# Finishing the memory projection inside the first feed-forward block, and splitting the fourth group's weights earlier

## The chip, the cores and the metric

The kernel runs on one core of one Trainium2 chip. The metric is the device time of one execution, in microseconds (us). Five engines work side by side, each through its own list of instructions in order: TensorE does the matrix products (PE in the profile, PEld for its weight loads), VectorE (DVE) and ScalarE (ACT) do elementwise work, GpSimd (POOL) does a few small operations, and SyncE (SP) issues most of the transfers from memory.

## The reference

A two-layer decoder trunk over 256 tokens of width 1024. A memory of 256 rows is normalised and projected once, and four cross-attention heads of each layer read it:

```
mem_kv = rms_norm(mem, mem_norm_g) @ mem_w_kv          # 256 x 1024: 512 columns of keys, 512 of values
for i in range(2):
    x = x + 0.5 * swiglu(rms_norm(x, ffn1_norm_g[i]), ffn1_w_in[i], ffn1_w_out[i])
    hn = rms_norm(x, mix_norm_g[i])
    # layer 0: mLSTM heads, layer 1: sliding-window attention; both with memory heads beside them
    # memory heads: q and k normalised per head, softmax(q k^T) v
    x = x + concat(y_tok, y_mem) @ w_out
    x = x + 0.5 * swiglu(rms_norm(x, ffn2_norm_g[i]), ffn2_w_in[i], ffn2_w_out[i])
```

`rms_norm` is `x * rsqrt(mean(x*x) + 1e-6) * g`. The memory's keys and values are first needed by the mixer of layer 0, behind the first feed-forward block.

## The kernel before, in words

Everything is kept in float32 accuracy by splitting each operand into a high part and a rest (`wh`, `wl` for weights, `xh`, `xl` for activations) and doing three products, `mm3` (lines 227 to 229: high by high, then two mixed ones). A weight tile is 128 by 1024 numbers, 512 KB. SP loads it into `wr` (line 220, five buffers), ACT casts it into `wh` (line 213), and DVE subtracts to get `wl` (line 214). One weight tile feeds 24 matmuls. Activations are split with their gain in the same way (`split_gain`: ACT line 134, DVE line 243).

A norm is applied after the product, since its factor is one number per token: `Norm.square` and `Norm.fold` sum the squares (ACT and DVE), `Norm.chain` sums over partitions by two small matmuls with `onesr` (line 303) and then takes the reciprocal root, for the memory's norm as two diagonals on DVE (line 294) and a power on POOL (line 308), for the residual's as a chain of operations on DVE (lines 314 to 322).

`memory()` runs first. It multiplies the memory, not yet normalised, by the key and value weights in four column groups of 256 (`Group` with `rows=True`): groups 1 and 2 give keys, groups 3 and 4 give values. In the kernel before, the memory's squares are taken while group 2 runs, the sum matmuls stand in group 3, and then, ahead of group 4, come the finishing steps: `head_norm` for both key groups straight from their PSUM banks, the copy of group 3 scaled by the norm (`vM`, line 134), and the split and squares of the residual `xT` (`x0.put`). Group 4's scaled copy follows. The keys are turned by four transposes a group (`turn`, line 238) and copied to `kT` (line 449). Then `ffn()` multiplies by the first feed-forward weights: 11 groups, each of four weight tiles and 96 matmuls; `hidden` reads the finished banks once `x0`'s norm is there (lines 501 to 504).

The order on PE and SP is that in which the program is written, with `Weave` slotting the spawned chains in when its own clock reaches their due time (the numbers in `LAT`). ACT and DVE are ordered by a list scheduler; `tc.issue_after(last[0].ins)` tells it to put instructions behind the last weight cast issued so far. PSUM has eight banks, taken in turn by `mo()`.

Of the kernel before, what the change touches and what calls it, by code (L numbers as in the profile page):

```python
# [10 lines left out]
F32 = mybir.dt.float32  # L11
# [3 lines left out]
AF = mybir.ActivationFunctionType  # L15
ALU = mybir.AluOpType
# [3 lines left out]
P = 128  # L20
# [12 lines left out]
def constants():  # L33
# [16 lines left out]

LAT = dict(pieces=1, norm=8.5, mnorm=3.5, x0=17.0, mkeys=7.2, cross=9.5, cross_s=1.5,
           cross_m=3.7, cross_p=8.7, cross_o=3.0, gates=20.0, scores=2.2, scores_m=8.4, num=6.9, num_r=7.5,
           keys=5.5, keys_d=7.2, query=9.0, head=1.5, head_m=2.5, head_p=9.3, head_o=4.0)

# [42 lines left out]
def tile_trunk(ctx: ExitStack, tc: tile.TileContext, a, out):  # L99
    nc = tc.nc  # L100
    seq = [0]

    def mk(pool, shape, dt, tag):
        seq[0] += 1
        return pool.tile(shape, dt, tag=tag, name=f"{tag}_{seq[0]}")
# [7 lines left out]
    wv = Weave()  # L113
# [19 lines left out]
    def act(*args, **kw):  # L133
        ins = nc.scalar.activation(*args, **kw)  # L134
        if args[2] not in (AF.Copy, AF.Square):
            tabled[0] = ins
# [6 lines left out]
    def unit(dt):  # L143
        return mk(up, [P, 2, T], dt, "u")

    def tmp():
        return mk(tp, [P, 2, T], F32, "t")
# [4 lines left out]
    def mo():  # L152
        return mk(pb8, [P, 512], F32, "bank")
# [47 lines left out]
    def g(i):  # L201
        return gcol[:, i:i + 1]


    pieces = [1]
    last = [None]
# [11 lines left out]
    def wtile(src, nk, ncol=256):  # L218
        raw = mk(wrp, [P, nk, ncol], F32, "wr")
        nc.sync.dma_start(raw, src)  # L220
        return split(raw, [P, nk, ncol])

    def wcols(w, c0, kh):
        return wtile(w.rearrange("(k p) f -> p k f", p=P)[:, kh * 4:(kh + 1) * 4, c0:c0 + 256], 4)
# [16 lines left out]
    def split_gain(src, gc, hi, lo):  # L241
        act(hi, src, AF.Copy, scale=gc)
        nc.vector.scalar_tensor_tensor(out=lo, in0=src, scalar=gc, in1=hi.bitcast(F32),
                                       op0=ALU.mult, op1=ALU.subtract)
# [9 lines left out]
    class Norm:  # L254
# [4 lines left out]
            self.done = False  # L259
            self.xT, self.xh, self.xl = [], [], []  # L260

        def put(self, xn):
            c2 = len(self.xT)
            hi, lo = mk(xhp, [P, 2, T], F32R, "xh"), mk(xlp, [P, 2, T], F32R, "xl")
            for m in range(2):
                split_gain(xn[:, m], g(self.gi + 2 * c2 + m), hi[:, m], lo[:, m])
            self.xh.append(hi)
            self.xl.append(lo)
            self.xT.append(xn)
            self.square(xn, c2 == 0)  # L270
            if c2 == 3:
                self.fold()

        def square(self, xn, first):
            if first:
# [108 lines left out]
    def head_scales(zc, hd, scaled):  # L384

        s2 = 1.0 / hd if scaled else 1.0
        e = mk(sp, [P, 2], F32, "qsc")
        nc.vector.tensor_scalar(e, zc, EPS / s2, None, op0=ALU.mult)
        return 1.0 / (hd * s2), e

    def head_factor(src, n, hsc):

        hd = src.shape[2] // n
        sq, v, u = tmp(), col(), col()
        sqv = sq[:, :, :n * hd]
# [26 lines left out]
    vM = mk(cst, [P, 2, 512], F32, "vM")  # L422
    x0 = Norm(G_F1)

    def memory():

        idle = tmp().rearrange("p a b -> p (a b)")[:, :T].bitcast(BF16)
        nc.vector.memset(idle, 0.0)
        bank = mo()
        for i in range(WARM):  # L430
            nc.tensor.matmul(bank, idle[:, :P], idle, start=True, stop=True, skip_group_check=True)
        wkv = a["mem_w_kv"]
        mh, ml, wfirst = [], [], []
# [12 lines left out]
        norm = Norm(G_MEM, rows=False)  # L446

        def keys(gi, kr):
            nc.scalar.copy(kT[gi], turn(kr))
            return  # L450
            yield

        for gi in range(2):
            gr = Group(wkv, gi * 256, mh, ml, rows=True)
            for kh in range(2):
                if gi == 0 and kh == 0:
                    yield from gr.first_part(wfirst[0])
                else:
                    yield from gr.part(kh, wfirst[kh] if gi == 0 else None)
            if gi == 0:  # L460
                first = gr
                continue
            nc.sync.dma_start(con, a["con"])
            with tc.issue_after(last[0].ins):
                for c2 in range(4):
                    norm.square(memT[c2], c2 == 0)
            norm.fold()
            wv.spawn(norm.chain(), LAT['mnorm'])
            gv = Group(wkv, 512, mh, ml, rows=True)
            yield from gv.all()  # L470
            for c2 in range(4):
                nc.sync.dma_start(xT[c2], a["xT"][:, 2 * c2:2 * c2 + 2])
            yield norm.ready
            hsc = head_scales(norm.zc, P, False)
            for i, q in enumerate((first, gr)):
                kr = tmp()
                head_norm(kr, q.ps, 2, hsc)
                wv.spawn(keys(i, kr), LAT['mkeys'] + 1.5 * i)
        for gi in range(2):
            if gi == 0:  # L480
                gr = gv
            else:
                gr = Group(wkv, 768, mh, ml, rows=True)
                yield from gr.all()
            for h in range(2):
                act(vM[:, h, gi * 256:(gi + 1) * 256], gr.ps[:, h], AF.Copy, scale=norm.rc[:, h:h + 1])
            if gi == 0:
                with tc.issue_after(last[0].ins):
                    for c2 in range(4):
                        x0.put(xT[c2])  # L490
                wv.spawn(x0.chain(), LAT['x0'])


    KG = [(0, 4), (4, 4), (8, 4), (12, 4), (16, 4), (20, 2)]
# [39 lines left out]
    def ffn(x, w_in, w_out, nxt=None, mid=None):  # L534
# [13 lines left out]
        for c2 in range(4):  # L548
# [25 lines left out]
            else:  # L574
                nxt.put(xn)
        wv.spawn(nxt.chain(), LAT['norm'])

# [15 lines left out]
    def cross_spawn(gr, gi, layer, hsc, ys):  # L593
# [5 lines left out]
        def queries():  # L599
# [456 lines left out]
```

## Time and profile before

| | |
|---|---|
| time, median of 3 runs | 1009.38 us (1009.06 to 1010.25) |
| profiled execution | 1010.58 us; its span, first to last instruction, 1008.7 us |
| busy time in the span | PE 996.2 us, PEld 978.1, DVE 664.4, ACT 531.0, POOL 29.7 |
| transferred | 182.70 MB |

The profiled execution is 1.9 us longer than its span; that is what lies around the instructions. Times in rows of the profile are counted from the span's start. "PEclk" is the granted TensorE clock as a share of full speed. A row of the timeline has the start, the length, the engine, the line, the operation, what it writes and reads, the shape, the count, and in brackets the idle time before it and what ended it.

### The profile page before, as it was taken

To read this page: it belongs to the slowest core of one execution; us is meant where nothing else is said; L and a number is where in the kernel's file an instruction comes from. 1 tells how busy PE (TensorE), PEld (TensorE's weight loads), DVE (VectorE), ACT (ScalarE), POOL (GpSimd) and SP (SyncE) were. 2 spreads that over 40 slices of the span, in tenths; PEclk is the share of its full clock that TensorE was granted. 3 is DMA by queue.
4 is the path that set the end of the run, shared out by engine and by line. 5 is a ranking of instruction groups with operands and counts; after the bars stand their busy time and mean duration, and the time that the engine had idled before them with its cause. 6 is when DMAs were issued, how large, how long until landed. Compare 5 with 4: busy or idle time off the path is not lost.

```text
span 1008.7 us, 20573 instructions
## 1 busy us (share of the span) xinstructions
PE 996.2 (99%) x8560; PEld 978.1 (97%) x8560; DVE 664.4 (66%) x1078; ACT 531.0 (53%) x779; POOL 29.7 (3%) x27
## 2 busy tenths in 40 slices
PE   8899999999999999999999999999999999999998
PEld 6899999999999999999999999999997899999998
DVE  6776665668766696666567665656777768666551
ACT  7654444446566464444445444455578755454440
POOL 1100000000100000000000000000132000000000
PEclk9999999999999999999999999999999999999999
DMA  9676656676634666665666666556641257666550
GB/s 307 197 250 197 195 180 195 185 190 194 189 126 136 185 191 199 190 195 180 198 193 201 201 192 191 186 180 200 205 148 50 88 157 223 193 192 187 187 168 22
DMA packets 173204, 182.70 MB, mean 181 GB/s; under 512 B 7124, under 2 KB 168328, under 8 KB 173112
## 3 DMA queue, kind: packets, MB, share of 16 engines
q1 hardware_dynamic: 171872, 179.60, 58.1%
q10 hardware_dynamic: 1016, 1.58, 0.5%
q8 instruction: 67, 1.10, 0.4%
q0 software_dynamic: 224, 0.22, 0.2%
q14 instruction: 25, 0.20, 0.1%
HBM read 180.32 MB, written 1.05 MB: 180 GB/s over the span
## 4 chain that ended last, share of the span: by engine, by line
PE 94%; ACT 2%; DVE 2%; DMA 1%; issue 0%; SPq 0%; POOL 0%; ACTq 0%; DVEq 0%
PE bank L227 30%; PE bank L229 30%; PE bank L228 30%; PE bank L233 2%; ACT u L134 1%; PE bank L238 1%; DMA wr<-in_mem_w_kv_dram 1%; DVE wl L214 1%; ACT wh L213 1%; PE bank L989 1%; DVE col L957 0%; PE bank L303 0%; DVE col L956 0%; SPq L435 0%; DVE u L248 0%
## 5 line engine op out<-in xcount | busy, mean ns | idle before, releaser
L214 DVE TENSOR_TENSOR wl<-wr,wh 128x1024 fp32r<-128x1024 f32 (+1 forms) x347 | 414.6, 1197 | 273.1 <-ACT wh L213 272.0
L213 ACT CAST wh<-wr 128x1024 fp32r<-128x1024 f32 (+1 forms) x347 | 356.7, 1032 | 389.8 <-PE bank L228 364.9
L227 PE MATMUL bank<-xh,wh 128*128 128x256 f32 x1544 | 427.8, 277 | 0.0
L228 PE MATMUL bank<-xl,wh 128*128 128x256 f32 x1544 | 426.4, 276 | 0.0
L229 PE MATMUL bank<-xh,wl 128*128 128x256 f32 x1544 | 426.4, 276 | 0.0
L227 PEld LDWEIGHTS bank<-xh,wh 128*128 128x128 f32 x1544 | 290.0, 188 | 0.1
L228 PEld LDWEIGHTS bank<-xl,wh 128*128 128x128 f32 x1544 | 289.9, 188 | 0.1
L229 PEld LDWEIGHTS bank<-xh,wl 128*128 128x128 f32 x1544 | 289.9, 188 | 0.0
L227 PE MATMUL bank<-u,wh 128*128 128x256 f32 x896 | 249.3, 278 | 0.0
L228 PE MATMUL bank<-u,wh 128*128 128x256 f32 x896 | 247.6, 276 | 0.0
L229 PE MATMUL bank<-u,wl 128*128 128x256 f32 x896 | 247.5, 276 | 0.0
L227 PEld LDWEIGHTS bank<-u,wh 128*128 128x128 f32 x896 | 168.2, 188 | 1.7 <-issue 1.7
L228 PEld LDWEIGHTS bank<-u,wh 128*128 128x128 f32 x896 | 168.3, 188 | 0.1
L229 PEld LDWEIGHTS bank<-u,wl 128*128 128x128 f32 x896 | 168.2, 188 | 0.0
L227 PE MATMUL bank<-wh,xh 128*128 128x256 f32 x208 | 59.6, 287 | 0.4 <-ACT t L982 0.4
L228 PE MATMUL bank<-wl,xh 128*128 128x256 f32 x208 | 57.9, 278 | 0.0
L229 PE MATMUL bank<-wh,xl 128*128 128x256 f32 x208 | 57.8, 278 | 0.0
L501 DVE TENSOR_TENSOR t<-bank,rb 128x256 f32<-128x256 f32 x88 | 36.4, 421 | 6.7 <-PE bank L229 6.7
L227 PEld LDWEIGHTS bank<-wh,xh 128*128 128x128 f32 x208 | 39.1, 188 | 1.1 <-ACT t L982 0.7
L228 PEld LDWEIGHTS bank<-wl,xh 128*128 128x128 f32 x208 | 39.0, 188 | 0.1
L229 PEld LDWEIGHTS bank<-wh,xl 128*128 128x128 f32 x208 | 39.0, 188 | 0.0
L134 ACT ACTIVATE u<-bank,col,col 128x256 f32<-128x256 f32 (+1 forms) x48 | 24.9, 530 | 15.2 <-DVE col L960 7.9
(180 smaller groups left out, 682.9 us busy)
## 6 DMA issues: line engine op xcount, KB each, us to landing
wr<-in_ffn_w_in_dram SPq DMA_DIRECT2D x176, 512.0 KB, 4.4
wr<-in_ffn_w_out_dram SPq DMA_DIRECT2D x80, 512.0 KB, 4.0
wr<-in_a_w_in_dram SPq DMA_DIRECT2D x28, 512.0 KB, 3.9
wr<-in_b_w_in_dram SPq DMA_DIRECT2D x14, 512.0 KB, 4.5
wr<-in_a_w_out_dram SPq DMA_DIRECT2D x12, 512.0 KB, 3.3
wr<-in_b_w_out_dram SPq DMA_DIRECT2D x12, 512.0 KB, 3.3
wr<-in_ffn_w_out_dram SPq DMA_DIRECT2D x16, 256.0 KB, 2.7
wr<-in_mem_w_kv_dram SPq DMA_DIRECT2D x7, 512.0 KB, 7.8
```

The lines of the kernel that those rows point to most:

```text
L134: ins = nc.scalar.activation(*args, **kw)
L213: last[0] = nc.scalar.copy(hi[:, i * n:(i + 1) * n], src[:, i * n:(i + 1) * n])
L214: tt(out=lo[:, i * n:(i + 1) * n], in0=src[:, i * n:(i + 1) * n], in1=hi[:, i * n:(i + 1) * n].bitcast(F32), op=ALU.subtract)
L227: nc.tensor.matmul(ps, wh, xh, start=start, stop=False, skip_group_check=True)
L228: nc.tensor.matmul(ps, wh, xl, start=False, stop=False, skip_group_check=True)
L229: nc.tensor.matmul(ps, wl, xh, start=False, stop=stop, skip_group_check=True)
L233: nc.tensor.matmul(ps, lhsT, rhs, start=start, stop=stop, skip_group_check=True)
L238: nc.tensor.transpose(ps, src, ident[:k, :k])
L501: tt(out=t[:, m], in0=ps[m][:, :T], in1=x.rb, op=ALU.mult)
L989: nc.tensor.matmul(o[es[e], cs], vr[:, i, js], pTs[e][:, src], start=i == 0, stop=i == 1, skip_group_check=True)
```

## The change

The finishing steps leave `memory()`'s run of four groups. Each group's bank is now copied raw, without any scale, by ACT (`late`): key groups into two `raw` tiles, value groups into `vM`. Group 4's two weight tiles are requested and split ahead of the residual's splits, which are then issued behind group 4's weight casts. The residual's squares and norm (`sums`), and the memory's squares, norm, scaling of `vM` in place, head norms of the keys and their transposes (`finish`) are chains of their own, slotted in while the first feed-forward block runs. `put` gets a flag to leave out the squares. Fifteen lines are added in all, so that lines 281 and up have other numbers after (285 is 286, 303 is 304, 501 is 516); lines 134 to 247 and 238 keep theirs.

```
-LAT = dict(pieces=1, norm=8.5, mnorm=3.5, x0=17.0, mkeys=7.2, cross=9.5, cross_s=1.5,
+LAT = dict(pieces=1, norm=8.5, mnorm=8.0, mrest=6.0, finish=18.0, raw=4.0, x0=2.5, fold=5.0, mkeys=7.2, cross=9.5, cross_s=1.5,
...
-        def put(self, xn):
+        def put(self, xn, square=True):
...
-            self.square(xn, c2 == 0)
-            if c2 == 3:
-                self.fold()
+            if square:
+                self.square(xn, c2 == 0)
+                if c2 == 3:
+                    self.fold()
...
+        def late(raw, gr):
+            with tc.issue_after(last[0].ins):
+                nc.scalar.copy(raw, gr.ps)
+            return
+            yield
+
+        def sums():
+            for c2 in range(4):
+                x0.square(xT[c2], c2 == 0)
+                yield 1.5
+            x0.fold()
+            yield LAT['fold']
+            yield from x0.chain()
+
+        def finish(raw):
+            for c2 in range(4):
+                norm.square(memT[c2], c2 == 0)
+                yield 2.0
+            norm.fold()
+            yield LAT['mnorm']
+            yield from norm.chain()
+            yield LAT['mrest']
+            for h in range(2):
+                nc.vector.tensor_scalar(vM[:, h], vM[:, h], norm.rc[:, h:h + 1], None, op0=ALU.mult)
+            hsc = head_scales(norm.zc, P, False)
+            for i in range(2):
+                yield 3.0
+                kr = unit(F32)
+                head_norm(kr, raw[i], 2, hsc)
+                wv.spawn(keys(i, kr), LAT['mkeys'])
+
-        for gi in range(2):
+        raw = [unit(F32) for _ in range(2)]
+        for gi in range(4):
             gr = Group(wkv, gi * 256, mh, ml, rows=True)
+            wts = [wcols(wkv, 768, kh) for kh in range(2)] if gi == 3 else wfirst if gi == 0 else [None] * 2
+            if gi == 3:
+                with tc.issue_after(last[0].ins):
+                    for c2 in range(4):
+                        x0.put(xT[c2], False)
             for kh in range(2):
                 if gi == 0 and kh == 0:
-                    yield from gr.first_part(wfirst[0])
+                    yield from gr.first_part(wts[0])
                 else:
-                    yield from gr.part(kh, wfirst[kh] if gi == 0 else None)
...
-            with tc.issue_after(last[0].ins):
                 for c2 in range(4):
-                    norm.square(memT[c2], c2 == 0)
-            norm.fold()
-            wv.spawn(norm.chain(), LAT['mnorm'])
...
-            yield norm.ready
-            hsc = head_scales(norm.zc, P, False)
-            for i, q in enumerate((first, gr)):
-                kr = tmp()
-                head_norm(kr, q.ps, 2, hsc)
-                wv.spawn(keys(i, kr), LAT['mkeys'] + 1.5 * i)
...
-            for h in range(2):
-                act(vM[:, h, gi * 256:(gi + 1) * 256], gr.ps[:, h], AF.Copy, scale=norm.rc[:, h:h + 1])
-            if gi == 0:
-                with tc.issue_after(last[0].ins):
-                    for c2 in range(4):
-                        x0.put(xT[c2])
-                wv.spawn(x0.chain(), LAT['x0'])
+                    yield from gr.part(kh, wts[kh])
+            dst = raw[gi] if gi < 2 else vM[:, :, (gi - 2) * 256:(gi - 1) * 256]
+            wv.spawn(late(dst, gr), LAT['raw'])
+            if gi == 1:
+                nc.sync.dma_start(con, a["con"])
+            if gi == 2:
                 for c2 in range(4):
-                    nc.sync.dma_start(xT[c2], a["xT"][:, 2 * c2:2 * c2 + 2])
...
+        wv.spawn(sums(), LAT['x0'])
+        wv.spawn(finish(raw), LAT['finish'])
```

The change shows in the order of instructions up to the end of the first feed-forward block's first product; behind that, the order on PE, ACT and DVE is the same before and after.

ACT before, around the casts of group 4's weights (`wh_464`, `wh_494`); `t_403` and `t_412` are squares of the key banks 200 and 249, `vM_128` the scaled copy of group 3:

```order
L134 ACTIVATE xh_439<-u_107,gcol_99 128x256 x2
L134 ACTIVATE xh_448<-u_108,gcol_99 128x256
L134 ACTIVATE t_403<-bank_200 128x512
L134 ACTIVATE xh_448<-u_108,gcol_99 128x256
L134 ACTIVATE vM_128<-bank_326,rc_382 128x256 x2
L213 CAST wh_464<-wr_462 128x1024
L134 ACTIVATE t_412<-bank_249 128x512
L213 CAST wh_494<-wr_492 128x1024
L213 CAST wh_528<-wr_526 128x1024
```

ACT after, in the same place: `wh_383` and `wh_389` are group 4's weights, `u_201` the raw copy of key bank 251, `acc_498` to `t_597` the residual's squares:

```order
L456 COPY u_201<-bank_251 128x512
L134 ACTIVATE acc_498<-u_105 128x512
L134 ACTIVATE t_531<-u_106 128x512
L134 ACTIVATE t_564<-u_107 128x512
L134 ACTIVATE t_597<-u_108 128x512
L213 CAST wh_383<-wr_381 128x1024
L247 CAST u_633<-acc_498 128x256
L213 CAST wh_389<-wr_387 128x1024
L134 ACTIVATE xh_393<-u_105,gcol_99 128x256 x2
L134 ACTIVATE xh_399<-u_106,gcol_99 128x256 x2
L134 ACTIVATE xh_405<-u_107,gcol_99 128x256 x2
L134 ACTIVATE xh_411<-u_108,gcol_99 128x256 x2
```

The residual's splits and the scaled copy have gone behind group 4's casts, the key squares are gone from here, and a raw copy and the residual's squares stand ahead of the casts. The next ACT rows after are the raw copy of group 3 and the first feed-forward cast, `wh_470`.

DVE after, from the sums of the residual's squares to the first feed-forward tile's rest, `wl_471` (group 4's are `wl_384`, `wl_390`; before, `wl_465` stood behind the memory's diagonals, both `L398`-`L399` steps of the first key group and `L408`, which waits for POOL):

```order
L282 TENSOR_TENSOR acc_498<-acc_498,t_531 128x512
L282 TENSOR_TENSOR acc_498<-acc_498,t_564 128x512
L282 TENSOR_TENSOR acc_498<-acc_498,t_597 128x512
L286 SCALAR_TENSOR_TENSOR acc_498<-acc_498 128x256
L214 TENSOR_TENSOR wl_384<-wr_381,wh_383 128x1024
L248 TENSOR_TENSOR u_633<-acc_498,u_633 128x256
L214 TENSOR_TENSOR wl_390<-wr_387,wh_389 128x1024
L243 SCALAR_TENSOR_TENSOR xl_394<-u_105,gcol_99,xh_393 128x256 x2
L243 SCALAR_TENSOR_TENSOR xl_400<-u_106,gcol_99,xh_399 128x256 x2
L243 SCALAR_TENSOR_TENSOR xl_406<-u_107,gcol_99,xh_405 128x256 x2
L243 SCALAR_TENSOR_TENSOR xl_412<-u_108,gcol_99,xh_411 128x256 x2
L214 TENSOR_TENSOR wl_471<-wr_468,wh_470 128x1024
```

What moved: no DVE row here waits for POOL or for a matmul of the memory's norm any more, and the whole split of the residual stands behind `wl_390`.

PE before, the transposes of the first key group; 24 matmuls of the first feed-forward product stand ahead of them:

```order
L228 MATMUL bank_525<-xl_431,wh_528 128x256
L229 MATMUL bank_525<-xh_430,wl_529 128x256
L238 MATMUL bank_556<-con_109,t_402 128x128 x4
L227 MATMUL bank_524<-xh_422,wh_564 128x256
L228 MATMUL bank_524<-xl_423,wh_564 128x256
```

PE after, the same transposes; 516 matmuls of the first feed-forward product stand ahead of them, and 36 more ahead of those of the second key group:

```order
L228 MATMUL bank_1204<-xl_400,wh_1238 128x256
L229 MATMUL bank_1204<-xh_399,wl_1239 128x256
L238 MATMUL bank_1254<-con_109,u_1134 128x128 x4
L227 MATMUL bank_1205<-xh_393,wh_1238 128x256
L228 MATMUL bank_1205<-xl_394,wh_1238 128x256
```

The first transposes moved back by 492 matmuls. The residual's sum matmuls (line 303, now 304) stand behind 168 of that block's matmuls instead of behind 108, and the memory's, which stood in group 3, now behind 348.

More of the change, by code (lines that the diff above doesn't have):

```diff
@@ L458, in memory @@
                 else:
-                    yield from gr.part(kh, wfirst[kh] if gi == 0 else None)
-            if gi == 0:
-                first = gr
-                continue
-            nc.sync.dma_start(con, a["con"])
-            with tc.issue_after(last[0].ins):
-                for c2 in range(4):
-                    norm.square(memT[c2], c2 == 0)
-            norm.fold()
-            wv.spawn(norm.chain(), LAT['mnorm'])
-            gv = Group(wkv, 512, mh, ml, rows=True)
-            yield from gv.all()
@@ L471, in memory @@
-            for c2 in range(4):
-                nc.sync.dma_start(xT[c2], a["xT"][:, 2 * c2:2 * c2 + 2])
-            yield norm.ready
-            hsc = head_scales(norm.zc, P, False)
-            for i, q in enumerate((first, gr)):
-                kr = tmp()
-                head_norm(kr, q.ps, 2, hsc)
-                wv.spawn(keys(i, kr), LAT['mkeys'] + 1.5 * i)
[L479 to L484, printed above, removed]
-            for h in range(2):
-                act(vM[:, h, gi * 256:(gi + 1) * 256], gr.ps[:, h], AF.Copy, scale=norm.rc[:, h:h + 1])
-            if gi == 0:
-                with tc.issue_after(last[0].ins):
-                    for c2 in range(4):
-                        x0.put(xT[c2])
-                wv.spawn(x0.chain(), LAT['x0'])
+                    yield from gr.part(kh, wts[kh])
@@ L494, in tile_trunk @@
+            dst = raw[gi] if gi < 2 else vM[:, :, (gi - 2) * 256:(gi - 1) * 256]
[3 more added lines that the diff above has]
+            if gi == 2:
+                for c2 in range(4):
+                    nc.sync.dma_start(xT[c2], a["xT"][:, 2 * c2:2 * c2 + 2])
+        wv.spawn(sums(), LAT['x0'])
+        wv.spawn(finish(raw), LAT['finish'])
     KG = [(0, 4), (4, 4), (8, 4), (12, 4), (16, 4), (20, 2)]
```

## Prediction

> **What bounds the kernel now.** I read the page first: busy time, then the chain that ended last.
>
> ```profile
> PE 996.2 (99%) x8560; PEld 978.1 (97%) x8560; DVE 664.4 (66%) x1078; ACT 531.0 (53%) x779; POOL 29.7 (3%) x27
> PE 94%; ACT 2%; DVE 2%; DMA 1%; issue 0%; SPq 0%; POOL 0%; ACTq 0%; DVEq 0%
> ```
>
> TensorE is the bound, and the change takes no matmul away. It can gain only where PE stands still or runs slowly. So next: PE's waits from 27.4 to 60 us, its timeline there, and the granted clock in neighbouring stretches of 3.41 us (columns: length, busy us and count of PE, PEld, DVE, ACT, POOL, then PEclk).
>
> ```profile
> PE bank L227 <- ACT wh L213: 2.0, 1, 2.0
> PE bank L228 <- DVE wl L214: 1.5, 1, 1.5
> ...
> 17.50 0.28 PE L229 MATMUL bank<-wh,u 128*128 128x256 f32 x1
> 23.15 0.28 PE L229 MATMUL bank<-wh,u 128*128 128x256 f32 x1
> 29.04 0.28 PE L229 MATMUL bank<-wh,u 128*128 128x256 f32 x1
> 31.29 0.39 PE L227 MATMUL bank<-wh,u 128*128 128x256 f32 x1 [1.98 <-ACT wh L213]
> 33.16 0.39 PE L228 MATMUL bank<-wl,u 128*128 128x256 f32 x1 [1.48 <-DVE wl L214]
> 40.22 0.28 PE L229 MATMUL bank<-wh,u 128*128 128x256 f32 x1
> 40.33 0.28 PE L227 MATMUL bank<-xh,wh 128*128 128x256 f32 x1
> 40.68 0.28 PE L227 MATMUL bank<-xh,wh 128*128 128x256 f32 x1
> ...
> 10.25:13.66 3.41, 1.88 (x12) 1.47 (x12) 2.43 (x5) 2.74 (x5) 0.00 (x0) 1.00 1.08 389
> 13.66:17.07 3.41, 3.41 (x18) 3.41 (x18) 3.41 (x5) 3.09 (x6) 0.00 (x0) 0.50 1.09 390
> 27.31:30.73 3.42, 2.00 (x18) 1.80 (x16) 2.44 (x10) 1.26 (x3) 1.56 (x2) 1.00 0.00 0
> 30.73:34.14 3.41, 1.37 (x9) 1.17 (x10) 2.86 (x4) 3.41 (x5) 0.52 (x1) 1.00 0.00 0
> 34.14:37.55 3.41, 3.41 (x18) 3.41 (x18) 2.51 (x5) 3.41 (x6) 2.49 (x2) 0.50 0.81 231
> ```
>
> Groups 1, 2 and 3 of the memory end with the matmuls that start at 17.50, 23.15 and 29.04. Group 4 should go on at 29.16, but its cast comes at 31.29 and its rest at 33.16. From 34.14 to 37.55 the clock is then half: 18 matmuls touch that stretch, where 31 would fit. The first feed-forward matmul starts at 40.33, that is 11.17 us for 48 matmuls. At 0.118 each (29.04 to 29.16 by its neighbours, and 4.83 us for 41 in the pace rows below) they take 5.65. So this place costs 5.5 us, of which 3.5 are the two waits and some 1.6 the half clock. The same table shows when the clock drops: a stretch in which PE was busy 1.88 or 1.37 of 3.41 us is followed by half clock, one with 2.00 is not.
>
> The Trainium skill ("TensorE: Matmul & The Clock Gate", the section on the HAM clock gate) puts the return to half rate behind an idle window of about 3.4 us. The stretch of 3.41 us and the factor 0.50 agree, but here stretches that were 40% and 55% busy sufficed. By the page's rule the spell at 34.14 would not come from these waits and would stay: the forecast below would be 1.6 us higher.
>
> **The change, part by part.** Durations come from the same execution. ACT, then DVE:
>
> ```profile
> 15.75 1.66 ACT L134 ACTIVATE t<-u 128x512 f32<-128x512 f32 x3
> 17.31 1.99 ACT L213 CAST wh<-wr 128x1024 fp32r<-128x1024 f32 x2
> 20.27 0.41 ACT L247 CAST u<-acc 128x256 fp32r<-128x256 f32 x1 [0.97 <-DVE acc L285]
> 20.58 0.91 ACT L134 ACTIVATE xh<-u,gcol 128x256 fp32r<-128x256 f32 x2
> 22.28 2.10 ACT L134 ACTIVATE xh<-u,gcol 128x256 fp32r<-128x256 f32 x5
> 24.27 0.58 ACT L134 ACTIVATE t<-bank 128x512 f32<-128x512 f32 x1
> 40.53 0.84 ACT L134 ACTIVATE vM<-bank,rc 128x256 f32<-128x256 f32 x2 [2.52 <-PE bank L229]
> ...
> 9.34 1.67 DVE L243 SCALAR_TENSOR_TENSOR u<-u,gcol,u 128x256 fp32r<-128x256 f32 x4
> 16.49 2.28 DVE L281 TENSOR_TENSOR acc<-acc,t 128x512 f32<-128x512 f32 x3
> 19.82 0.42 DVE L285 SCALAR_TENSOR_TENSOR acc<-acc 128x256 f32<-128x256 f32 x1
> 20.15 1.22 DVE L214 TENSOR_TENSOR wl<-wr,wh 128x1024 fp32r<-128x1024 f32 x1
> 31.89 1.22 DVE L214 TENSOR_TENSOR wl<-wr,wh 128x1024 fp32r<-128x1024 f32 x1
> ```
>
> Instructions of one engine overlap a little, so I go from start to start: a square takes 0.52 (15.75 to 17.31 for three), a cast of a tile 0.95, an `xh` piece 0.40 (22.28 to 24.27 for five), a copy of a bank 0.48 (0.58 less the tenth that the others overlap), a sum's cast 0.31 (20.27 to 20.58). A reader of a bank begins 0.03 after the last matmul's end (40.22 + 0.28, ACT at 40.53); a matmul 0.05 after its `wl` (31.89 + 1.22 = 33.11, matmul at 33.16).
>
> The raw copies are a new wait: each stands in ACT's queue until PE ends its group, and everything behind it waits too. The first starts at 17.50 + 0.31 = 17.81; behind it the casts of group 3 end at 20.3 and their rests on DVE (1.2 each) at 21.8, while group 3 begins at 23.27 and needs its second tile at 26.1: covered by 3 us. The second copy starts at 23.15 + 0.31 = 23.46. Then four squares (2.08) give 26.02, and the cast `wh_383` ends at 27.07; group 4 needs it at 23.27 + 48 x 0.118 = 28.92: covered by 1.8 us. On DVE the three sums start when the second square is done (25.1) and take 2.28, then the fold 0.33, so `wl_384` runs from 27.8 to 29.05. It is needed at 29.04 plus nothing: a wait of 0 to 0.2 us. Group 4's second tile: the cast of the folded sum waits for the fold (28.0) and takes 0.31, `wh_389` ends at 29.3, `wl_390` at 30.6, needed at 31.7. So the large wait goes.
>
> What is late next is the first feed-forward tile. Behind `wh_389` ACT does eight `xh` pieces (29.25 + 3.2 = 32.45) and the raw copy of group 3 (32.95); `wh_470` ends at 34.0 and DVE, done with the `xl` pieces (eight at 0.42 behind 30.5) at 33.85, does `wl_471` from 34.03 to 35.25. PE comes to the first feed-forward matmul at about 34.75, and the third, which reads `wl_471`, would start at 34.99; it starts at 35.29. Another tenth goes in refilling, as behind 33.16. The fourth matmul then starts at 35.5, where before it started at 40.68: a gain of 5.2 us. Both ends of that: 5.5 + 0.2 if neither wait shows, and 4.2 if ACT's or DVE's steps take a further microsecond. The memory's two sum matmuls, which stood in group 3, move into the later product and come off it: 0.23 us (the two at 53.59 below). The half clock at 34.14 goes with the waits: no stretch of 3.41 us is then left with under 2.9 busy. That at 13.66 stays, as nothing moves ahead of 17 us.
>
> Transfers are asked for in the same order; a `wr` buffer is freed by its `wl`, and `wl_384` and `wl_390` now come 3 us earlier than 31.89 and on, so the loads behind them are not late. Removed: two scaled copies on ACT (0.84 each) for two raw ones (0.6), nothing on the path. Added: two raw key copies, and `vM` times its factor on DVE, 128x512 twice. No row shows that operation; the nearest are 0.42 (L285, half as large) and some 0.76 (L281): 1 to 1.5 us, in the feed-forward block where DVE is two thirds busy.
>
> That block has to absorb all the finishing work. Its margins, counted from the fourth matmul at 35.5: the residual's sum matmuls come after 168 matmuls, at about 55; nine DVE steps as large as L285 (0.42 to 0.5 one behind the other), three `wl` that wait for freed buffers and the copies of the factor end at 62, the first `hidden` has read its banks at about 66, and PE needs those banks again at 288 matmuls, 69. The memory's sum is ready at 70, needed at 76; the first turned keys are ready at 87, needed at 96. So I cost them at nothing; with the cover gone, a PE wait there would be a few tenths to 3 us.
>
> **The pace of the matmuls.** There is a price that the order hides. PE's timeline, around the transposes and the residual's sum:
>
> ```profile
> 38.09 0.28 PE L229 MATMUL bank<-wh,u 128*128 128x256 f32 x1
> 42.92 0.28 PE L228 MATMUL bank<-xl,wh 128*128 128x256 f32 x1
> 43.16 0.60 PE L238 MATMUL bank<-con,t 128*128 128x128 f32 x4
> 46.10 0.28 PE L227 MATMUL bank<-xh,wh 128*128 128x256 f32 x1
> 53.47 0.28 PE L229 MATMUL bank<-xh,wl 128*128 128x256 f32 x1
> 53.59 0.39 PE L303 MATMUL bank<-u,onesr 128*128 128x256 f32 x2
> 53.81 0.28 PE L227 MATMUL bank<-xh,wh 128*128 128x256 f32 x1
> 256.45 0.28 PE L228 MATMUL bank<-wl,xh 128*128 128x256 f32 x1
> 731.88 0.60 PE L238 MATMUL bank<-con,u 128*128 128x128 f32 x4
> 732.44 0.28 PE L228 MATMUL bank<-wl,xh 128*128 128x256 f32 x1
> 733.38 0.28 PE L227 MATMUL bank<-wh,xh 128*128 128x256 f32 x1
> ```
>
> From 38.09 to 42.92 there are 41 steps, 0.1178 us each, all at full clock and with nothing waited for. From 46.10 to 53.47 there are 65, 0.1134 each. The long pace holds from the first group on and through both waits; the short one begins right behind the first four transposes at 43.16 and goes on, past the sum at 53.59, to 256.45. So in this trace the pace has two values that persist, and in the memory and the first feed-forward block only the transposes changed it. After the change the first transposes stand behind 516 feed-forward matmuls instead of 24: 492 matmuls at the long pace, 492 x 0.0044 = 2.15 us lost. The bounds of this term: 0 if the short pace begins at once, and all some 1880 matmuls from 43.5 to 256.5, 8.3 us, if the later transposes do not bring it. I take 2.15, since what ends the long pace in this block is one thing in the trace, and the sum at 27.5 us in group 3 did not.
>
> **Sum.** 5.2 - 0.23 - 2.15 = 2.8 us. The profiled execution becomes 1010.58 - 2.8 = 1007.8. It stood 1.2 above the median of the three runs, so against that median: 1009.38 - 2.8 = 1006.6 us, a ratio of 0.9972.
>
> **Rivals.** First, the short pace comes early, by the short wait at 35 or by the sum matmuls: then 0 to 0.6 us of the 2.15 are lost, and the time is 1004.4 to 1005.0. For it: the pace can be short for 200 us, past a sum. Against it: both long waits before (31.29 and 33.16) left it long at 38.09. Second, slower: the transposes at 516 and 552 leave the pace long, as those at 731.88 did, behind which 732.44 to 733.38 is eight steps of 0.1175. Then it stays until 256, 8.3 us are lost, and the time is 1009.38 - 4.97 + 8.3 = 1012.7. It decides from 1130 matmuls at the long pace on, that is if it lasts to about 170 us. Against it: those at 731.88 stood in a product with weights as the moving operand; the four at 43.16 stood in the very product that follows here, and there are two such sets. Third, half clock still comes between 29 and 38 us, as the page's rule would leave it, or because the short waits fall badly: 1.6 us more, 1008.2. The table of stretches speaks against it. Fourth, the finishing work delays the feed-forward block or the ACT chain ahead of group 4 by 1 to 2.5 us more than counted: 1007.6 to 1009.1, which is no change within what can be measured.
>
> **How the numbers follow.** The forecast has 62%, the early short pace 13%, the lasting long pace 8%, half clock 7%, delays 10%. About 0.2% (2.0 us) is what can be told from no change, so faster means under 1007.4 and slower over 1011.4. The forecast's own spread is about 0.8 us (the 4.2 to 5.7 of the first term, and the runs' own 1.2), which leaves some 54 of its 62 points under 1007.4; with the early pace and a little of the rest, faster has 68%. Slower is the lasting long pace, 8%; the same 24%. The range leaves out the lasting pace and the ends of the others: 1004.4 to 1009.0.
>
> **What would show it.** Right: PE goes from the memory's last group into the feed-forward block with under 1 us of waits, `PEclk` stays 1.00 from 20 us on, the fourth feed-forward matmul starts near 35.5, steps are 0.118 until the four transposes near 96 us and 0.113 behind them. Wrong: a step of 0.113 at 40 us already (then faster than said), or 0.118 at 150 us (slower); a wait of PE on `wl` above 0.5 us near 29 or 35; a wait on a bank near 69 us, or on the turned keys near 96.

## The result, and the profile after

| | before | after |
|---|---|---|
| time, median | 1009.82 us (1009.06 to 1010.80, 4 runs) | 1004.31 us (1003.73 to 1005.52, 4 runs) |
| ratio | | 0.9946 (0.9934 to 0.9958) |
| profiled execution | 1010.58 us, span 1008.7 | 1004.76 us, span 1003.0 |

The change made the kernel 5.5 us faster (4.2 to 6.7 by the interval), where 2.8 had been forecast. An execution can have spells of half clock (3.41 us each; the profile before has two, a first at 13.66 and one behind group 4's waits at 34.14), and which it has differs from run to run, so profiles with the same first spell are compared below too.

The page of after, its busy row, and PE's waits up to 300 us (engine and line, what it waited for, then us in total, times, longest):

```profile
PE 993.9 (99%) x8560; PEld 975.7 (97%) x8560; DVE 664.6 (66%) x1080; ACT 531.9 (53%) x779; POOL 29.4 (3%) x27
...
PE bank L432 <- DVE t L429: 1.4, 1, 1.4
PE bank L228 <- DVE wl L214: 0.9, 1, 0.9
PE bank L227 <- ACT wh L213: 0.4, 1, 0.4
```

The two waits of 2.0 and 1.5 us at group 4 are not in this list any more; the three that are left stand ahead of 14 us. Now the same stretches and the same places as before (stretches: length, busy us and count of PE, PEld, DVE, ACT, POOL, then PEclk, DMA share and GB/s):

```profile
9.83:13.24 3.41, 2.25 (x15) 1.66 (x13) 2.68 (x5) 2.32 (x5) 0.00 (x0) 1.00 1.08 388
13.24:16.65 3.41, 3.26 (x27) 3.26 (x28) 3.41 (x6) 2.13 (x3) 0.00 (x0) 1.00 1.08 388
30.31:33.72 3.41, 3.39 (x29) 3.18 (x28) 3.17 (x7) 3.35 (x6) 0.00 (x0) 1.00 0.61 184
20.00:250.00 230.00, 229.89 (x2016) 229.61 (x2015) 165.46 (x242) 128.56 (x165) 4.32 (x4) 1.00 0.68 206
```

```profile
27.40 0.28 PE L229 MATMUL bank<-wh,u 128*128 128x256 f32 x1
...
27.66 0.38 PE L228 MATMUL bank<-wl,u 128*128 128x256 f32 x1
...
33.30 0.28 PE L227 MATMUL bank<-xh,wh 128*128 128x256 f32 x1
33.42 0.28 PE L228 MATMUL bank<-xl,wh 128*128 128x256 f32 x1
33.81 0.38 PE L229 MATMUL bank<-xh,wl 128*128 128x256 f32 x1
34.03 0.28 PE L227 MATMUL bank<-xh,wh 128*128 128x256 f32 x1
34.50 0.28 PE L228 MATMUL bank<-xl,wh 128*128 128x256 f32 x1
53.35 0.28 PE L229 MATMUL bank<-xh,wl 128*128 128x256 f32 x1
53.47 0.40 PE L304 MATMUL bank<-u,onesr 128*128 128x256 f32 x2
53.94 0.28 PE L229 MATMUL bank<-xh,wl 128*128 128x256 f32 x1
60.17 0.28 PE L227 MATMUL bank<-xh,wh 128*128 128x256 f32 x1
93.38 0.60 PE L238 MATMUL bank<-con,u 128*128 128x128 f32 x4
```

Four readings. First, the fourth feed-forward matmul starts at 34.03, where it started at 40.68: 6.65 us earlier. Second, no stretch between 20 and 250 us is at half clock, and PE is busy for 229.89 of those 230 us: nothing that was moved into the feed-forward block makes PE wait. Third, this execution has no half clock at 13.24 either; the stretch ahead of it was 2.25 us busy, where before it was 1.88. Nothing that the change moved stands there, so this part of the gain is luck (the run of the changed kernel again, below, has that spell). Fourth, from 34.50 to 53.35 there are 160 steps of 0.1178 us, the long pace; from 53.94 to 60.17, behind the residual's sum matmuls at 53.47, there are 55 of 0.1133. So the long pace ended 40 us ahead of the transposes at 93.38.

Where DVE now stands ahead of the feed-forward block (start, length, engine, line, operation; in brackets the idle time before it):

```profile
26.39 1.22 DVE L214 TENSOR_TENSOR wl<-wr,wh 128x1024 fp32r<-128x1024 f32 x1
...
32.53 2.36 DVE L214 TENSOR_TENSOR wl<-wr,wh 128x1024 fp32r<-128x1024 f32 x2 [0.24 <-ACT wh L213]
```

The first row is `wl_384`, ready at 27.61, and the matmul that reads it starts at 27.66 with a wait of 0.02 us. The last is `wl_471` and the next: the first of them is ready at about 33.7, and the matmul at 33.81 started 0.27 us late for it (PE itself stood still for 0.11 of that, since the matmul before it ran until 33.70). Both are the small waits that the prediction had put there.

### The profile page after: what moved, and what is told of

It is laid out like the page before. It is cut to its first block, busy times and chain, and to the rows that moved or that the text cites. A ratio compares the mean times of both kernels' runs of the same rounds, so it can differ in the third digit from the quotient of the medians.

```text
span 1003.0 us, 20581 instructions
## 1 busy us (share of the span) xinstructions
PE 993.9 (99%) x8560; PEld 975.7 (97%) x8560; DVE 664.6 (66%) x1080; ACT 531.9 (53%) x779; POOL 29.4 (3%) x27
## 4 chain that ended last, share of the span: by engine, by line
PE 93%; ACT 3%; DVE 2%; DMA 1%; issue 0%; SPq 0%; ACTq 0%; DVEq 0%
PE bank L227 30%; PE bank L229 30%; PE bank L228 30%; PE bank L233 2%; ACT u L134 1%; PE bank L238 1%; ACT wh L213 1%; DMA wr<-in_mem_w_kv_dram 1%; DVE wl L214 1%; PE bank L1004 1%; ACT xh L134 0%; DVE col L972 0%; DVE acc L282 0%; PE bank L304 0%; DVE col L971 0%
```

## The experiments

What was open: why 5.5 us and not 2.8, that is what each part is worth, what the first half-clock spell has to do with it, and what ends the long pace (steps of 0.1178 us instead of 0.1133). The theory throughout: the gain is the waits and half clock around group 4 (5.2 us), less the matmuls moved off (0.23), less what the long pace costs, plus the chance of the first spell.

**The changed kernel again** (`after_again`), unchanged, beside the others.

> The changed kernel as it is, more runs of it. Theory 1: two kinds of runs about 1.5 us apart, the longer with a mean clock 0.002 lower; over more runs the gain on the kernel before comes down from 5.5 towards 4.3 to 4.8 us. Theory 2: it stays at 5.5 us.

Measured: 1005.70 us (1004.12 to 1006.39, 5 runs), ratio 0.9954 (0.9941 to 0.9968), that is 4.6 us; the medians of that comparison differ by 3.9 (1009.60 over 15 runs of the kernel before). Its profile caught the first spell:

```profile
10.10:13.51 3.41, 1.94 (x12) 1.32 (x11) 2.49 (x5) 2.81 (x6) 0.00 (x0) 1.00 1.08 389
13.51:16.92 3.41, 3.41 (x16) 3.41 (x17) 3.22 (x5) 1.65 (x2) 0.00 (x0) 0.50 1.09 389
...
35.63 0.29 PE L227 MATMUL bank<-xh,wh 128*128 128x256 f32 x1
54.95 0.28 PE L229 MATMUL bank<-xh,wl 128*128 128x256 f32 x1
55.07 0.40 PE L304 MATMUL bank<-u,onesr 128*128 128x256 f32 x2
```

This is the like-for-like pair to the profile before, which had that spell too. The fourth feed-forward matmul starts at 35.63 (forecast 35.5), 5.05 us earlier than before. From 35.63 to 54.95 there are 164 steps of 0.1178, and the sum at 55.07 ends the long pace again. The spans differ by 1008.7 - 1004.6 = 4.1 us.

**Filling the first wait**, in the kernel before (`fill_before`) and in the changed one (`fill_after`): five more of the kernel's 512-column warm-up matmuls around the first matmul of group 1's second tile, where PE waits for its rest (the row at 13.10 below shows what is left of that wait).

```
+        def fill(n):
+            for i in range(n):
+                nc.tensor.matmul(bank, idle[:, :P], idle, start=True, stop=True, skip_group_check=True)
...
                     yield from gr.first_part(wts[0])
+                    fill(2)
...
+                    yield from gr.part(kh, wts[kh], (lambda: fill(3)) if gi == 0 else None)
```

The function handed to `part` is called inside `mm3`, behind the first matmul of the tile.

> The kernel before, with five more warm-up matmuls (512 columns, 0.22 us each) put where PE waits at 11.4 to 13.3 us for group 1's second weight tile, two ahead of the tile's first matmul and three behind it. They feed nothing. Theory 1 (the half-clock spell at 13.66 us of the before profile is a matter of how the free stretches of 3.41 us fall on those two waits; it belongs to neither kernel, and the change is worth 5.2 - 0.23 - 0.63 = 4.3 us): the spell never comes, so this kernel runs at the fast end of the kernel before, 1008.5 to 1009.4 us, with a small spread. Theory 2 (the change itself is worth the whole 5.5 us that the medians show, without such luck): no change of the median beyond 0.4 us, 1009.4 to 1010.2.

> The changed kernel with the same five matmuls. Theory 1: the profile of the changed kernel had no such spell, so nothing is gained against its fast runs: 1003.7 to 1004.8 us, and 4.0 to 4.7 us under the kernel before with the same fill. Theory 2: 5.5 us under the filled kernel before.

Measured: `fill_before` 1009.29 us (1008.52 to 1010.67, 11 runs), ratio 0.9999 (0.9990 to 1.0008); `fill_after` 1003.99 us (1003.73 to 1004.23, 5 runs), ratio 0.9944 (0.9931 to 0.9956). In the changed kernel the fill did what was meant: all five runs have a mean clock of 1.000 and lie within 0.5 us, where five of the changed kernel alone lay within 2.3. In the kernel before the spread stayed at 2 us, which was not expected; four of its eleven runs show a mean clock of 0.996 or 0.997, where one spell makes 0.998. The idle end of a run can be at half clock too (in the profile before from 1006.94 to 1008.70, worth about 0.001), so the one run at 0.997 may have one spell or two; the three at 0.996, by this estimate, have two. Where the second lies no profile shows; the one taken is of a run at 0.998, with one spell, from 31.4 us. A rival to the wait at 11 to 13 us is group 4's place itself. That is an estimate from this profile: two neighbouring stretches that begin at 25.70 and 29.11 would be only 1.57 and 1.79 us busy there, which could make two spells behind those waits alone.

So theory 1 held for `fill_after` by itself (1003.7 to 1004.8), but not for the small spread of `fill_before`, and not for the difference of the two: the filled medians lie 5.3 us apart, where 4.0 to 4.7 was forecast. The difference from the forecast's 4.3 is in part the pace: in the profile of `fill_after` it is short from the start of the feed-forward block, which is worth 0.6 us against the changed kernel. The profile of `fill_after` (timeline, then stretches):

```profile
11.46 0.61 PE L439 MATMUL bank<-t 128*128 128x512 bf16 x2
12.07 0.82 PE L439 MATMUL bank<-t 128*128 128x512 bf16 x3
13.10 0.39 PE L230 MATMUL bank<-wl,u 128*128 128x256 f32 x1 [0.21 <-DVE wl L214]
...
8.21:11.62 3.41, 3.39 (x21) 2.73 (x22) 3.06 (x7) 2.59 (x5) 0.00 (x0) 1.00 1.05 351
11.62:15.03 3.41, 3.20 (x22) 2.33 (x21) 3.21 (x5) 2.99 (x5) 0.00 (x0) 1.00 1.08 387
```

Both stretches are at least 3.2 us busy, and full clock follows. Its matmuls are at the short pace from 34.2 us on already.

**The hoist alone** (`hoist_only`): the kernel before, with group 4's two tiles split ahead of the head norms and the residual's splits, and nothing else moved.

```
+            w4 = [wcols(wkv, 768, kh) for kh in range(2)]
             yield norm.ready
...
-                yield from gr.all()
+                for kh in range(2):
+                    yield from gr.part(kh, w4[kh])
```

> The kernel before, with one part of the change alone: group 4's two weight tiles are requested and split ahead of the head norms and of the residual's splits; the finishing steps stay in the memory part, and the transposes stay early. Theory 1 (the rest of group 4's first tile waits on DVE behind a head norm that waits for POOL, and what is put behind comes late for the first feed-forward tile): PE still waits about 3 us for the first wl of group 4 (to about 32.4 us instead of 33.2) and then about 5 us for the first feed-forward wl (to about 43.8 us): 3 us slower than before, about 1012.5. Theory 2 (the weights' place is what gained, the finishing steps could have stayed): 3 to 5 us faster, 1005 to 1006.

Measured: 1013.94 us (1012.96 to 1015.46, 4 runs), ratio 1.0044 (1.0030 to 1.0058): 4.4 us slower, where theory 1 had 3. PE's waits from group 4 on, then DVE and two stretches:

```profile
PE bank L228 <- DVE wl L214: 2.9, 1, 2.9
PE bank L227 <- ACT wh L213: 1.9, 1, 1.9
PE bank L229 <- DVE wl L214: 0.8, 1, 0.8
...
28.95 0.69 DVE L408 TENSOR_TENSOR t<-bank,col 128x512 f32<-128x512 f32 x1 [1.12 <-POOL col L401]
29.56 1.22 DVE L214 TENSOR_TENSOR wl<-wr,wh 128x1024 fp32r<-128x1024 f32 x1
...
27.82:31.23 3.41, 0.52 (x5) 0.40 (x4) 2.29 (x4) 3.31 (x7) 1.00 (x1) 1.00 0.00 0
38.05:41.47 3.42, 0.81 (x4) 0.61 (x5) 3.10 (x6) 3.39 (x6) 0.00 (x0) 1.00 0.00 0
```

The rest of group 4's tile still stands behind the key heads' step that waits for POOL (28.95), so its wait is 2.9 us; and the residual's splits, now behind group 4's casts, make the first feed-forward tile 2.7 us late. The waits sum to 5.6 us where they were 3.5, and each of the two nearly empty stretches is followed by half clock (0.50 in the stretches from 31.23 and from 41.47). The finishing steps, not the order of the casts alone, held group 4 back.

**The finishing steps alone** (`finish_only`): the changed kernel with group 4's tiles split where `part` asks for them, behind the residual's splits.

```
-            wts = [wcols(wkv, 768, kh) for kh in range(2)] if gi == 3 else wfirst if gi == 0 else [None] * 2
+            wts = wfirst if gi == 0 else [None] * 2
```

> The changed kernel with the other part alone: the finishing steps stay in the feed-forward block, but the residual's splits stand ahead of group 4's weight casts, as in the kernel before. Theory 1 (most of the gain is that DVE no longer waits for POOL and for the memory's norm; the weights' place is worth what eight splits take on DVE less the slack): group 4's first wl comes about 1.5 us late instead of 0.02, the wait for the first feed-forward wl (0.27 us) is gone, so PE's fourth feed-forward matmul is 1.2 us later than in the changed kernel and the time 1005.2 to 1006.5, up to 1.6 us more in runs in which that wait brings a half-clock spell. Theory 2 (both parts are needed, neither gains by itself): 1008 us or more.

Measured: 1005.35 us (1004.84 to 1005.91, 4 runs), ratio 0.9955 (0.9939 to 0.9971).

```profile
27.90 0.38 PE L227 MATMUL bank<-wh,u 128*128 128x256 f32 x1 [0.21 <-ACT wh L213]
29.16 0.39 PE L228 MATMUL bank<-wl,u 128*128 128x256 f32 x1 [0.88 <-DVE wl L214]
```

The waits at group 4 come back at 1.1 us in all, the wait at the first feed-forward tile is gone, and no half clock follows. All four runs have a mean clock of 1.000; the changed kernel's four runs with 1.000 (of nine) have a mean of 1004.12. So beside the finishing steps the hoist is worth about 1.2 us, and without them it costs 4.4.

**What ends the long pace.** Six kernels, all from the changed one. `z_early`, `z_156`, `z_192`: the residual's sum matmuls stand behind 120, 156 or 192 feed-forward matmuls instead of 168 (`fold` in `LAT` 0.0, 3.0 or 8.0 instead of 5.0); `z_early_2` is `z_early` again, letter for letter. `pairs_rows` puts two spare matmuls of `onesr` by an activation ahead of group 3 and two behind the sixth feed-forward matmul, `single` one behind the sixth and three behind the 102nd, all into a bank that is overwritten afterwards:

```
+    def spare(ps, n, mv):
+        for i in range(n):
+            nc.tensor.matmul(ps, onesr, mv, start=True, stop=True, skip_group_check=True)
```

> The changed kernel with one number changed: the residual's sum matmuls (line 304) stand behind 120 feed-forward matmuls instead of 168. Theory P1 (two sum matmuls in a stream with activations moving end the long pace of 0.118 us; in a stream with weights moving they leave or bring the long one): steps are 0.118 until those two matmuls and 0.113 right behind them, 48 matmuls earlier, 0.2 us gained. Theory P2 (the pace is drawn anew, by chance of timing, at any break): it may change there or not. Theory P3 (the pace changes with time or with the block's progress, not with these matmuls): it still changes near 53.9 us, behind 168.

> The changed kernel with two pairs of extra matmuls by onesr (128x256, overwritten by the real products, nothing waits for them): one pair ahead of group 3 of the memory, where weights move, and one behind six matmuls of the first feed-forward group, where activations move. Theory P1: the pace stays 0.118 behind the first pair and is 0.113 from the second pair on, at about 34 us, so the fourth part of 1 us is lost less: 0.6 us gained, 0.47 us paid for the four matmuls. Theory P2: either pair may change it. Theory P3: no change before 53.9 us.

> The kernel with the residual's sum behind 120 feed-forward matmuls, once more. In its first profile the pace was long from 34 us on and stayed long past this sum, and changed at the memory's sum, behind 348. In all profiles so far, one weight load of three is 0.192 us long in the long pace and 0.188 otherwise. Theory P4: the sum ends the long pace where the long load is that of line 227, of line 304 or of line 229, and not where it is that of line 228; which one it is, is left by the last wait. P2: the pace behind a sum has nothing to do with that.

> The residual's sum behind 156 feed-forward matmuls. P4: short pace behind it, unless the long load is that of line 228. P2: either. P3 (the block's progress): no change before 168.

> The residual's sum behind 192 feed-forward matmuls. P4 as above; if the long pace ends there, it was long for 24 matmuls more than in the changed kernel (0.1 us). P3: the change comes at 168, ahead of the sum.

> The changed kernel with one extra matmul by onesr behind six feed-forward matmuls and three behind 102 (128x256, overwritten by the real products). Theory P4: each of them can end the long pace, by which load is the long one; one matmul does as well as two or three. Theory P5 (only two in a row with the same weights end it): the single one changes nothing, the three do.

One profiled execution each, so the times themselves decide nothing (one spell more or less outweighs what is looked for): `z_early` 1005.18, `pairs_rows` 1005.76, `z_early_2` 1005.48, `z_156` 1003.52, `z_192` 1004.12, `single` 1004.42 us. First PE in `z_early`, then in `z_early_2`:

```profile
34.11 0.28 PE L228 MATMUL bank<-xl,wh 128*128 128x256 f32 x1
47.30 0.28 PE L229 MATMUL bank<-xh,wl 128*128 128x256 f32 x1
47.42 0.40 PE L304 MATMUL bank<-u,onesr 128*128 128x256 f32 x2
47.90 0.28 PE L229 MATMUL bank<-xh,wl 128*128 128x256 f32 x1
60.50 0.28 PE L228 MATMUL bank<-xl,wh 128*128 128x256 f32 x1
74.52 0.40 PE L304 MATMUL bank<-u,onesr 128*128 128x256 f32 x2
```

```profile
35.94 0.28 PE L228 MATMUL bank<-xl,wh 128*128 128x256 f32 x1
48.63 0.28 PE L229 MATMUL bank<-xh,wl 128*128 128x256 f32 x1
48.75 0.39 PE L304 MATMUL bank<-u,onesr 128*128 128x256 f32 x2
```

In `z_early` the steps are 0.1178 before the sum at 47.42 (112 of them) and behind it (107 from 47.90 to 60.50), and they stay so until the memory's sum at 74.52. In `z_early_2`, the same program, 112 steps of 0.1133 lead to the same sum: the pace was short from the first wait of the feed-forward block on. It was short from there in `z_156`, `z_192` and `fill_after` too, and long in the profiles of `after`, `after_again`, `finish_only` and `z_early`. Behind that wait the pace takes about five steps to settle (in `z_156` 0.222, 0.118, 0.122, 0.116, 0.114, then 0.113). The spare matmuls behind the sixth feed-forward matmul, in `pairs_rows` at 35.87 and in `single` at 34.31, fall into that settling; the pace behind them is short, and whether they made it so is not shown. The first pair of `pairs_rows`, at 23.33 in group 3, left the pace long. In `fill_before` the sum in that group even began it: 0.1133 up to 25.35, 0.1176 behind it. So in the memory's groups the long pace is not a fixture either.

So a sum does not always end the long pace (it did not at 47.42), nor does a given amount of progress in the block. A third idea was that it depends on which of the three weight loads is the longer one, 0.192 us instead of 0.188, when the sum comes; it fits the six sums that were met in the feed-forward block while the pace was long, but the four last runs could not try it, since the pace was short before any sum came. In the memory's groups no load is the longer one in the long pace (187 to 188 ns each in `before` and `hoist_only`), so there the sign is missing. What chooses the pace behind a wait stays open. It is not the program alone, as `z_early` and `z_early_2` show.

**The parts together** (`best`): the changed kernel with the fill, with two spare matmuls behind the sixth feed-forward matmul, and with the third and fourth split of the residual behind the first feed-forward tile's cast.

```
-                    for c2 in range(4):
+                    for c2 in range(2):
                         x0.put(xT[c2], False)
...
                     wh, wl = wcols(w_in, part * FF + gi * 256, kh)
+                    if len(x.xh) == 2:
+                        with tc.issue_after(last[0].ins):
+                            for c2 in range(2, 4):
+                                x.put(xT[c2], False)
```

> A version meant to beat both: the changed kernel, with the five filling matmuls at 11 to 13 us, the pair by onesr behind six feed-forward matmuls, and the residual's third and fourth split put behind the first feed-forward tile's cast and rest, so that wl of that tile does not come late (0.27 us of wait and 0.1 of refill). Theory 1 and P1: the filled changed kernel (1003.99) less 0.35, and no more than 0.24 paid for the pair, since the pace there was short anyway: 1003.4 to 1004.1 us. If the third and fourth split come late instead, a wait near 39 us: 1004.5 us.

Measured: 1003.67 us (1003.39 to 1004.16, 5 runs), ratio 0.9941 (0.9928 to 0.9954).

```profile
32.80 0.29 PE L227 MATMUL bank<-xh,wh 128*128 128x256 f32 x1
33.04 0.28 PE L231 MATMUL bank<-xh,wl 128*128 128x256 f32 x1
33.49 0.39 PE L236 MATMUL bank<-xh,onesr 128*128 128x256 f32 x2
```

In `best` the third feed-forward matmul starts 0.24 us behind the first (0.51 in the changed kernel): the wait for `wl_471` is gone. The steps go from 0.118 to 0.113 at 33.15, three matmuls ahead of the spare pair at 33.49 and with no wait in front: here the pair did not end the long pace. The version has the lowest median of the versions with more than one run, by 0.6 us under the changed kernel's median in the first comparison and 0.3 under `fill_after`, which is within the spread of the runs.

## Why the prediction was wrong, point by point

The time, 1004.31, came out 0.1 below the range's low end and 2.3 below the forecast. The waits and the clock behind them were right; the term for the pace was mis-sized because its rule was wrong, and one outcome was taken as fixed that differs from run to run.

- **The waits and the half clock, 5.2 us: right.** In `after_again`, which has the first spell as the profile before has, the fourth feed-forward matmul came 5.05 us earlier. The small waits that were to be next came where and as large as said, and `finish_only` shows that the hoist is worth about 1.2 us of it.
- **The finishing work costs nothing: right.** PE stood still for 0.11 of 230 us from 20 us on. The fourth rival (delays) is out.
- **The half clock at 34 goes: right**, and the third rival is out: no profile of the changed kernel shows it. The Trainium skill's condition, an idle window ("TensorE: Matmul & The Clock Gate", the section on the HAM clock gate), is not what the rows show: 1.37, 1.88 and 1.94 of 3.41 us busy, none of them idle, were each followed by half clock. But the prediction's own reading, that the busy time of a stretch tells when the clock drops, does not hold either. In `z_early_2` 2.04 us busy was followed by half clock; in the kernel before 2.00 was not, and in `z_192` 1.78 was not (below first `z_early_2`, then `z_192`, each time the stretch and the one behind it; the stretches of `z_192` are counted back from the fall of its clock at 1001.14 us, in steps of 3.4133):

```profile
9.92:13.34 3.42, 2.04 (x13) 1.44 (x12) 2.60 (x6) 2.56 (x5) 0.00 (x0) 1.00 1.08 389
13.34:16.75 3.41, 3.41 (x16) 3.41 (x17) 3.26 (x5) 1.70 (x2) 0.00 (x0) 0.50 1.08 388
```

```profile
751.97:755.38 3.41, 1.78 (x15) 0.95 (x13) 2.70 (x13) 3.32 (x13) 0.00 (x0) 1.00 0.00 0
755.38:758.80 3.42, 3.42 (x27) 2.61 (x26) 2.27 (x10) 1.50 (x7) 0.00 (x0) 1.00 0.00 0
```

What the Trainium skill says in that section of a free-running window agrees with two profiles in which PE had the same two waits at 11 to 13 us: 0.58 and 0.88 in `after_again`, 0.57 and 0.88 in `z_156`. In the first one stretch, 10.10 to 13.51, holds both (1.94 busy) and half clock follows; in the second the stretches are cut at 12.31, are 2.83 and 2.53 busy, and no half clock follows. In `after` the first of these waits was shorter as well, 0.43.

- **The pace, 2.15 us: this step failed.** "In the memory and the first feed-forward block only the transposes changed it" was read off one trace, and "the sum at 27.5 us in group 3 did not" off one event in it. In the profiled execution of the changed kernel the residual's sum ended the long pace after 168 matmuls: (168 - 24) x 0.0044 = 0.63 us lost, not 2.15. In six profiles of the changed kernel's close variants (`fill_after`, `best`, `z_early_2`, `z_156`, `z_192`, `single`) the short pace stood within the block's first ten matmuls, and this term is near 0. In `hoist_only` the second set of transposes even began a long pace: six steps of 0.113 ahead of it, then 71 of 0.1178 from 47.76 to the sum at 56.12. What chooses the pace stays open. The first rival, an early short pace, was the right one in its mechanism; it had 13%, against 62% for the forecast. That its 1004.4 to 1005.0 us also came near is in part luck: it counted on the first spell, and the runs with that spell have a mean of 1005.83.
- **"That at 13.66 stays": only in some runs.** The nine runs of the changed kernel fall, by mean clock, into 4 at 1.000 (mean 1004.12 us), one at 0.999 (1004.57) and 4 at 0.998, that is with one spell (1005.83). Three of the four in the first comparison had none, so its 5.5 us lie on the high side. The 25 runs of the kernel before fall into 9 at 0.998, with one spell (1009.11), 7 at 0.996, with two (1010.16), and 9 at 0.997, which can be either (1010.07). Where the second spell lies is known from one profile alone, and `fill_before` has runs at 0.996 although the wait at 11 to 13 us is filled there. With one spell less in the changed kernel than before, runs differ by 1009.11 - 1004.12 = 5.0 us, or by 1010.16 - 1005.83 = 4.3; over all runs of both the gain is 1009.75 - 1004.93 = 4.8 us.

The account of the two profiles that both have the first spell (`before` and `after_again`): 5.05 for the waits and the half clock, -0.23 for the two matmuls moved off, -0.63 for the pace, 4.2 in all; their spans differ by 4.1.

## What to carry to other kernels

Price a wait on the bound engine together with the clock behind it: here 3.5 us of waits took another 1.6 through the stretch that followed. Splitting a tile earlier pays only if nothing that waits stays ahead of it in any of the queues it passes: the same hoist cost 4.4 us with the finishing steps in place and gained about 1.2 without them. And what one trace shows once (which pace, which spell, from which busy share the clock drops) is one draw: give it a spread, not a rule, until a second profile of the same program shows it again.

## What the runs showed of the hardware that was not expected

- A stream of loads and matmuls of 256 columns has two paces at full clock, 0.1133 and 0.1178 us, each lasting for up to hundreds of steps (347 in `z_early`), and the same program can take either behind the same wait (`z_early` and `z_early_2`). In `z_early` the long one cost 347 x 0.0045 = 1.6 us. Single events changed it both ways: a sum ended it in `after` and began it in `fill_before`.
- Half clock does not need an idle stretch, and PE's busy time in a stretch of 3.41 us does not decide it alone: 1.94 and 2.04 us were followed by it, 1.78 and 2.00 were not. What else decides is open. Five filling matmuls in a 1.5 us wait kept it away in all five runs of `fill_after`.
